# A two-layer hybrid backbone: adaLN pieces in groups run from the last loaded on, and a last projection laid out by tokens

## The chip, the cores and the metric

The kernel runs on one core of a Trainium2 chip. The metric is the time of one execution on the device in microseconds (us); lower is better. PE is the matmul engine (TensorE), DVE is VectorE, ACT is ScalarE, POOL is GpSimd and SP is SyncE; the last two issue nearly all DMAs here.

## The reference

Two layers work on 512 tokens (256 context, 256 latent) of width 2048, all in float32. Per layer, `c @ ada_w` gives a shift, a scale and a gate per feature for latent and context (adaLN); the normed and modulated tokens go through one input projection into three head groups (an S5 state space, attention with 8 heads, an mLSTM), and the joined outputs go through the output projection and are added through the gate. The second layer keeps the latent tokens only, and the result is a final RMSNorm.

```
shift, scale, gate = split(silu(c) @ ada_w[l] + ada_b[l], 3)
xn = rmsnorm(h_lat, norm_w[l]) * (1 + scale) + shift
ya, yb, yc = s5(xn @ w_in), attention(xn @ w_in), mlstm(xn @ w_in)
h_lat = h_lat + gate * (concat([ya, yb, yc]) @ w_out[l])
...
return rmsnorm(h_lat, final_norm_w)
```

## The kernel before

Activations lie with features on the 128 partitions and tokens along the free axis (16 tiles `h` of 128 x 512). Each matmul in the projections is made of three: every weight chunk of 128 x 1024 is loaded by SP (`wchunk`, L178 on, three buffers `raw`), split by ACT into a high part `hi` and by DVE into a rest `lo`, and the activations likewise into `xh` and `xl`; `hi*xh`, `hi*xl` and `lo*xh` are added up in PSUM. A tile scheduler orders the instructions of each engine by priorities; within an engine they run in that order, so one that waits holds up all behind it.

The stages are, in order: the first loads, S5 preparation of layer 0 (`s5_prep`, DVE) and row statistics (`st`, `sp`, `spb` on PE); `inputs` (L1204 on), which makes the modulated tokens two tiles at a time (`make_xn`) and feeds them into the S5 projection (`proj_u`, tiles `pu`), the attention values (`pv`) and the gates (`gps`); `layer`; `out_proj` of layer 0; then the same for layer 1.

The adaLN vectors of layer 0 come from 64 pieces of weights, 512 KB each, in groups of four. POOL loads a piece into one of five buffers `ar` (L287); PE multiplies it by the two-column `cact` into `adps` (`ada_piece`, four matmuls that are eight records in the trace, L159), and after the fourth piece of a group ACT copies the sum out (`aev`) and two small matmuls turn it to columns (`ada_flush`). `ada_step(1)` stands between every three `pu` matmuls, and each call runs one piece. Each piece that is run lets POOL load the next one. The gates of layer 0 are 32 such pieces that run during the attention projections (`ada_open` with `batch=BT0`). The adaLN vectors of layer 1 are made on DVE instead, in the mLSTM stage of layer 0: 64 pieces of 512 KB in two buffers, two multiply-reduces `aj` each (`adv_piece`, L368).

`out_proj` (L1386 on) of layer 1 makes 16 feature tiles of 128 x 256: 48 matmuls of 256 columns each, the weights stationary. Then the gate is applied (`h`), squares are summed over partitions by PE (`st`), and at the end the root of the mean is computed, spread by a matmul (`spb`), and multiplied in before the four output DMAs.

Of the kernel before, what the change touches and what calls it, by code (L numbers as in the profile page):

```python
# [52 lines left out]
BT0 = 1  # L53
# [66 lines left out]
PC = dict(ada_b=(0, 48), nw=(48, 16), cw=(64, 24), cb=(88, 8), mnw=(96, 4), gb=(100, 1), fw=(101, 16), qkw=(117, 2))  # L120
NPC = 119


class Kern:
# [126 lines left out]
    def proj_u(self, l, i, ada):  # L251
# [6 lines left out]
        for kk in range(2):  # L258
            k = 2 * i + kk
            wh, wl = hi[:, kk * 512:kk * 512 + 512], lo[:, kk * 512:kk * 512 + 512]  # L260
            for t in range(4):
# [5 lines left out]
                if ada:  # L267
                    self.ada_step(1)

# [20 lines left out]
    def ada_piece(self, pid):  # L290


        self.ada_flush()
        ps, raw = self.ada_ps, self.ada_raw.pop(pid)
        fine = pid < 64
        pc, last = (pid % 4, 3) if fine else (pid % 16, 15)
        for j in range(4):
            self.mm(ps[32 * j:32 * j + 2, 0:256], self.cact[:, 4 * pc + j if fine else pc],
                    raw[:, j * 256:j * 256 + 256], start=pc == 0, stop=pc == last)
        if pc < last:  # L300
            return
        ev = self.aq["ev"]()
        self.act(ev, ps[:, 0:256], AF.Copy)
        self.apend = (pid, ev)
# [21 lines left out]
    def ada_open(self, pool, bufs, rate, ids, tag="ar", ev=None, batch=1):  # L326
# [3 lines left out]
                       src="ada", run=self.ada_piece)  # L330
        self.ada_fetch()

    def adv_open(self, pool, bufs, rate, ids):
# [3 lines left out]
                       src="adt", run=self.adv_piece)  # L337
# [63 lines left out]
    def ada_next(self):  # L401
        q = self.aq
        q["run"](q["ids"][q["done"]])
# [53 lines left out]
    def make_xn(self, l, pool, hb, rb, ks):  # L457

        xt = []
        for k in ks:  # L460
            t = pool.tile([128, 512], F32, tag="xt", bufs=5, name=self.nm("xt"))
# [33 lines left out]
    def s5_prep(self, l, sp, dp, scratch):  # L495
        V = self.V
        g = self.s5 = {}
        par = sp.tile([128, 112], F32, name=self.nm("spar"))
        self.nc.sync.dma_start(par, self.i["spar"][l])
# [101 lines left out]
        bt = scratch("b", [128, 2, 16, 16])  # L601
        self.nc.sync.dma_start(bt, self.i["sb"][l].rearrange("p (r a q) -> p r a q", r=2, a=16))
# [382 lines left out]
    def ml_gates(self, l):  # L985
# [16 lines left out]
        li = mp.tile([128, 4, 2, 4], F32, tag="ga6", bufs=1, name=self.nm("ga"))  # L1002
# [19 lines left out]
        RQ = mp.tile([128, 128], F32, tag="RQ", bufs=1, name=self.nm("RQ"))  # L1022
        bt = mp.tile([128, 128], F32, tag="bt", bufs=1, name=self.nm("bt"))
# [181 lines left out]
    def inputs(self, l, pool, hb, rb, ada=False):  # L1205
# [3 lines left out]
        xt = []  # L1209
        for i in range(8):  # L1210
            if ada:
                while self.aq["done"] < 8 * i + 8:
                    self.ada_step(1)
                if self.aq["done"] == 8 * i + 8:
                    self.ada_flush()
            ks = (2 * i, 2 * i + 1)
            xt += self.make_xn(l, pool, hb, rb, ks)
            self.proj_u(l, i, ada)
# [17 lines left out]
    def layer(self, l, sp):  # L1236
# [73 lines left out]
        if need:  # L1310
            self.adv_open(mp, 2, ADR, range(0, 64))
# [74 lines left out]
    def out_proj(self, l, hp, beside=lambda: None, side=()):  # L1386

        need = l == 0
        t0 = 0 if need else NCTX
        n = NT - t0  # L1390
        self.pri = 400
        hb, self.hw, sq = [], [], {}

        def group(a):
            for k in range(a, a + 4):
                self.stats_add(k, sq.pop(k), n)

        self.stats_begin()
        for dt in range(KT):
            h = hp.tile([128, 512], F32, tag=f"h{dt}", bufs=1, name=self.nm("h"))  # L1400
            src = self.i["ht"][dt] if need else self.hs[dt]
            self.nc.sync.dma_start(h[:, t0:], src)

            def cb(ps):
                for v, a in ((1, 0), (0, 256)) if need else ((0, 256),):
                    hh = h[:, a:a + 256]
                    self.stt(hh, ps[:, a - t0:a - t0 + 256], self.adG[l][:, dt, v:v + 1], hh, OP.mult, OP.add)
                if need:
                    self.nc.sync.dma_start(self.hs[dt], h[:, 256:512])
                    return  # L1410

            self.pri, self.epri = 400, 400
            self.proj_a((self.i["wo"][l, dt, 0], self.i["wo"][l, dt, 1]), t0, cb)
# [5 lines left out]
            sq[dt] = self.stats_sq(hp, h[:, t0:], n, "xt", 5)  # L1419
            if not need and dt:  # L1420
                self.final_w(hp, hb, dt - 1)
        beside()
        group(12)
        if not need:
            self.final_w(hp, hb, 15)
        return hb

    def final_w(self, hp, hb, dt):
        if dt % 4 == 0:
# [175 lines left out]
```

## Time and profile before

| | |
|---|---|
| median of 3 runs | 1658.59 us (1657.88 to 1662.95) |
| the profiled execution | 1657.79 us |
| its span in the trace | 1656.0 us, so 1.79 us lie around it |
| PE busy | 1588.6 us, 96% of the span |
| DVE, ACT, POOL busy | 73%, 40%, 8% |

The matmuls overlap in the trace (a 512-column one lasts 0.39 us and the next starts 0.23 us later), so a busy PE is not a PE at its peak: the distance between starts tells what a matmul costs. Rows of the timeline give the start and the length in us, the engine, the line, the output and the operands, and how many were merged (`x8`).

### The profile page before, as it was taken

What the parts mean: (1) busy time and instruction counts of PE and PEld (TensorE: products, weight loads), DVE (VectorE), ACT (ScalarE), POOL (GpSimd) and SP (SyncE); (2) the same over time, 40 slices, a digit from 0 to 9 for tenths busy, and PEclk for the clock granted to TensorE, in tenths of its full rate; (3) what the DMA queues carried; (4) which work ended last, traced back from release to release, by engine and by line L of the source; (5) the groups of instructions that cost most, each with busy time, mean ns of one, the idle gap of its engine ahead of it and who ended that gap; (6) DMA issues with size and microseconds to landing.
All of it is one profiled execution on the core that took longest, in us unless ns stands there. A gap on an engine that the chain in (4) does not pass through costs nothing.

```text
span 1656.0 us, 27071 instructions
## 1 busy us (share of the span) xinstructions
PE 1588.6 (96%) x10542; PEld 1346.8 (81%) x10542; DVE 1203.6 (73%) x2545; ACT 669.3 (40%) x1278; POOL 131.2 (8%) x252
## 2 busy tenths in 40 slices
PE   5999999999999899999999999899999999999996
PEld 1567988878768878788887777689989979999996
DVE  5432888777949796999899887556777687557744
ACT  3333344434354344322242323463355453354542
POOL 2221010010000110110000110100000012000000
PEclk9999999999999999999999999899999999999998
DMA  9885244351225665565455555535455458553753
GB/s 378 299 302 175 87 141 168 128 181 52 66 104 165 187 194 179 179 200 183 137 171 168 188 184 171 185 99 165 155 184 172 157 188 279 193 161 118 223 178 112
DMA packets 88033, 288.08 MB, mean 174 GB/s; under 512 B 10208, under 2 KB 18144, under 8 KB 87264
## 3 DMA queue, kind: packets, MB, share of 16 engines
q1 hardware_dynamic: 52704, 158.33, 29.5%
q0 software_dynamic: 35200, 128.01, 23.1%
q8 instruction: 83, 1.36, 0.3%
q14 instruction: 46, 0.38, 0.1%
HBM read 268.44 MB, written 17.86 MB: 173 GB/s over the span
## 4 chain that ended last, share of the span: by engine, by line
PE 61%; DVE 18%; issue 12%; DMA 7%; ACT 2%; POOL 0%; DVEq 0%; POOLq 0%; ACTq 0%
PE pa L159 28%; PE pb L159 9%; PE pu L159 6%; DMA ar<-adt 5%; DVE lo L145 4%; DVE tp L145 3%; PE adps L159 3%; PE psm L159 2%; DMA ar<-ada 2%; DVE aj L368 2%; PE psY L159 2%; PE pv L159 2%; PE psO L159 1%; PE psS L159 1%; DVE S L785 1%
## 5 line engine op out<-in xcount | busy, mean ns | idle before, releaser
L159 PE MATMUL pa<-xh,hi 128*128 128x512 f32 (+1 forms) x1408 | 490.3, 348 | 0.0
L156 ACT ACTIVATE hi<-raw 128x1024 fp32r<-128x1024 f32 x256 | 271.1, 1059 | 539.1 <-PE pa L159 307.4
L159 PE MATMUL pa<-xh,lo 128*128 128x512 f32 (+1 forms) x1408 | 484.6, 344 | 0.0
L159 PE MATMUL pa<-xl,hi 128*128 128x512 f32 (+1 forms) x1408 | 484.4, 344 | 0.0
L145 DVE TENSOR_TENSOR lo<-raw,hi 128x1024 fp32r<-128x1024 f32 x256 | 312.6, 1221 | 143.5 <-ACT hi L156 136.7
L159 PEld LDWEIGHTS pa<-xh,hi 128*128 128x128 f32 x1408 | 266.4, 189 | 34.7 <-issue 5.4
L159 PEld LDWEIGHTS pa<-xh,lo 128*128 128x128 f32 x1408 | 266.7, 189 | 31.1 <-issue 1.9
L159 PEld LDWEIGHTS pa<-xl,hi 128*128 128x128 f32 x1408 | 266.8, 189 | 30.7 <-issue 2.7
L159 PE MATMUL pb<-hi,xh 128*128 128x256 f32 x832 | 241.7, 291 | 0.0
L159 PE MATMUL pb<-lo,xh 128*128 128x256 f32 x832 | 238.3, 286 | 0.0
L159 PE MATMUL pb<-hi,xl 128*128 128x256 f32 x832 | 237.7, 286 | 0.0
L368 DVE CUSTOM_DVE_ANT_0 aj<-ar,cb 128x1024 bf16<-128x1024 f32 x160 | 195.3, 1220 | 33.8 <-DMA ar<-adt 32.5
L159 PEld LDWEIGHTS pb<-hi,xh 128*128 128x128 f32 x832 | 160.1, 193 | 4.4 <-issue 4.1
L159 PEld LDWEIGHTS pb<-lo,xh 128*128 128x128 f32 x832 | 160.3, 193 | 1.9 <-issue 1.0
L159 PEld LDWEIGHTS pb<-hi,xl 128*128 128x128 f32 x832 | 160.1, 192 | 2.0 <-issue 2.0
L287 POOL DMA_DIRECT2D ar<-adt x96 | 50.7, 528 | 545.3 <-DVE adp L368 216.8
L159 PE MATMUL adps<-ar,cact 128*2 128x256 f32 x768 | 67.3, 402 | 18.1 <-DVE cact L145 12.1
L287 POOL DMA_DIRECT2D ar<-ada x96 | 50.7, 529 | 314.7 <-PE adps L159 310.6
L159 PE MATMUL pu<-hi,xh 128*128 128x512 f32 x128 | 56.4, 440 | 4.1 <-ACT xh L156 4.1
L156 ACT ACTIVATE g<-psS,sm 128x512 f32<-128x512 f32 (+1 forms) x48 | 29.3, 611 | 62.9 <-DVE sm L149 62.4
L159 PE MATMUL pu<-lo,xh 128*128 128x512 f32 x128 | 54.5, 426 | 0.0
L159 PE MATMUL pu<-hi,xl 128*128 128x512 f32 x128 | 53.8, 429 | 0.0
(301 smaller groups left out, 2155.9 us busy)
## 6 DMA issues: line engine op xcount, KB each, us to landing
raw<-wa SPq DMA_DIRECT2D x112, 512.0 KB, 3.6
ar<-ada POOLq DMA_DIRECT2D x96, 512.0 KB, 5.1
ar<-adt POOLq DMA_DIRECT2D x96, 512.0 KB, 4.3
raw<-wb SPq DMA_DIRECT2D x64, 512.0 KB, 3.9
raw<-wo SPq DMA_DIRECT2D x64, 512.0 KB, 3.6
raw<-wu SPq DMA_DIRECT2D x16, 512.0 KB, 4.4
h<-ht SPq DMA_DIRECT2D x32, 256.0 KB, 6.0
tb<-E POOLq DMA_DIRECT2D x8, 516.0 KB, 3.2
```

What stands on the lines that cost most here:

```text
L145: return self.V.tensor_tensor(o, a, b, op=op)
L156: return self.S.activation(o, a, f, **kw)
L159: return self.T.matmul(o, w, x, start=start, stop=stop, skip_group_check=True)
L287: self.nc.gpsimd.dma_start(raw, self.i[self.aq["src"]][pid])
L368: self.V.tensor_tensor_reduce(junk, raw, row, 1.0, 0.0, OP.mult, OP.add, self.adp[:, half, kind, dt, v:v + 1])
L785: V.tensor_tensor_scan(f(S[:, ri]), f(dt), f(Z[:, ri]), 0.0, op0=OP.mult, op1=OP.add)
```

## The change

- `ada_open` gets a run order: with `batch=4` each group of four pieces is run back to back, the one loaded last first, and the group's first and last matmul flags follow. Seven buffers take the place of five. The gates of layer 0 run in twos (`BT0 = 2`).
- The first loads are issued in another order (S5 parameters, constants, then the 16 `h`), and they, the opening of the adaLN pieces and `s5_prep` get a higher priority than the statistics.
- `inputs` makes the modulated tokens of step i+1 during step i (`ready`, called from `proj_u`); the buffers of `xt` grow from 5 to 7 (layer 0) and 6 (layer 1).
- The DVE pieces of layer 1's adaLN get a third buffer in layer 0; to make room, three small tiles of the mLSTM gates share others.
- The last output projection is written anew (`out_last`): tokens on partitions, the activations stationary and 512 weight columns moving. The gate row comes from a matmul with ones (`pg`), the residual `hs` is turned by PE (`ph`), squares are summed by ACT along the free axis, and the final weight is a row tile (`fw`).

```diff
-BT0 = 1
+BT0 = 2
+XTB = (7, 6)
@@ proj_u
                 if ada:
                     self.ada_step(1)
+                if kk == 0 and t == 0:
+                    ahead()
@@ ada_piece
-        pc, last = (pid % 4, 3) if fine else (pid % 16, 15)
+        n, b = 4 if fine else 16, self.aq["batch"]
+        pc, first, last = pid % n, b - 1, n - b
...
-                    raw[:, j * 256:j * 256 + 256], start=pc == 0, stop=pc == last)
-        if pc < last:
+                    raw[:, j * 256:j * 256 + 256], start=pc == first, stop=pc == last)
+        if pc != last:
@@ ada_open, ada_next
+        self.aq["order"] = [p for a in range(0, len(ids), batch) for p in reversed(ids[a:a + batch])]
...
-        q["run"](q["ids"][q["done"]])
+        q["run"](q["order"][q["done"]])
@@ inputs
+        def ready(i):
+            if i > 7:
+                return
             if ada:
                 while self.aq["done"] < 8 * i + 8:
                     self.ada_step(1)
...
+            with self.tc.high_priority(60):
+                xn[i] = self.make_xn(l, pool, hb, rb, (2 * i, 2 * i + 1))
+        ready(0)
...
+            self.proj_u(l, i, ada, lambda: ready(i + 1))
@@ layer
-            self.adv_open(mp, 2, ADR, range(0, 64))
+            self.adv_open(mp, 3, ADR, range(0, 64))
@@ out_last (new, in place of out_proj(1), final_w and stats_end)
+        def gate(b):
...
+            self.tt(dg, self.c("I").unsqueeze(1).to_broadcast([128, 4, 128]),
+                    self.adG[1][:, 4 * b:4 * b + 4, 0:1].to_broadcast([128, 4, 128]), OP.mult)
+            pg = self.pS.tile([128, 512], F32, tag="bS", name=self.nm("pg"))
+            self.mm(pg, self.c("ONE"), dg.rearrange("p a c -> p (a c)"))
+            self.act(gr[:, 512 * b:512 * b + 512], pg, AF.Copy)
+        for b in range(4):
...
+            for ch in range(8):
...
+                for t in range(2):
+                    for kk in range(2):
...
+                        self.mm(ps[t], self.xh[k][:, tk], wh, start=k == 0, stop=False)
+                        self.mm(ps[t], self.xh[k][:, tk], wl, start=False, stop=False)
+                        self.mm(ps[t], self.xl[k][:, tk], wh, start=False, stop=k == 15)
...
+                    self.tr(p[:, 128 * q:128 * q + 128], hs[4 * b + q][:, 128 * t:128 * t + 128])
...
+                    self.tt(o, ps[t], gr[:, bs], OP.mult)
+                    self.tt(o, o, pt[t], OP.add)
+                    self.act(sq, o, AF.Square, accum_out=ss[:, t, b:b + 1])
+                    if b < 3:
+                        self.tt(o, o, fw[:, bs], OP.mult)
+        self.V.tensor_reduce(ms, ss, axis=AX.X, op=OP.add)
+        self.ts(ms, ms, 1.0 / D, OP.mult, EPS, OP.add)
+        self.rsqrt(hp, rs, ms, 2)
+        for t in range(2):
+            self.stt(H[t][:, 1536:], H[t][:, 1536:], r, fw[:, 1536:], OP.mult, OP.mult)
+            self.act(H[t][:, :1024], H[t][:, :1024], AF.Copy, scale=r)
+            self.ts(H[t][:, 1024:1536], H[t][:, 1024:1536], r, OP.mult)
...
@@ body
+            with tc.high_priority(1000):
...
+                ids = range(64)
+                self.ada_open(hp, 7, 1.0, ids, batch=4)
+                self.s5_prep(0, s5c, s5c, scratch, loads)
```

The order of PE just ahead of the first `pu` matmul, before (`ar` are adaLN pieces, `st`, `sp` and `spb` the statistics):

```order
L159 MATMUL adps<-ar_410,cact 2x256 x4
L159 MATMUL sp_500<-cst,sev_498 128x2 x4
L159 MATMUL adps<-ar_419,cact 2x256 x4
L159 MATMUL adps<-ar_428,cact 2x256 x4
L159 MATMUL adps<-cst,aev_479 128x2 x2
L159 MATMUL adps<-ar_439,cact 2x256 x4
L159 MATMUL spb_535<-dg_533,cst 128x512
L159 MATMUL adps<-ar_452,cact 2x256 x4
L159 MATMUL adps<-ar_461,cact 2x256 x4
L159 MATMUL adps<-ar_470,cact 2x256 x4
L159 MATMUL pu_574<-hi_580,xh_562 128x512
```

The same place now:

```order
L160 MATMUL st_323<-sq_454,cst 32x512
L160 MATMUL adps<-cst,aev_441 128x2 x2
L160 MATMUL sp_489<-cst,sev_487 128x2 x4
L160 MATMUL adps<-ar_423,cact 2x256 x4
L160 MATMUL adps<-ar_402,cact 2x256 x4
L160 MATMUL adps<-ar_394,cact 2x256 x4
L160 MATMUL adps<-ar_388,cact 2x256 x4
L160 MATMUL spb_539<-dg_537,cst 128x512
L160 MATMUL adps<-cst,aev_483 128x2 x2
L160 MATMUL pu_562<-hi_568,xh_550 128x512
```

Seventeen pieces stood ahead of `spb` and three between it and the first `pu`; now sixteen stand ahead of it, the last four in falling order, and none behind it.

PE during the S5 projection, before:

```order
L159 MATMUL pu_576<-hi_580,xh_562 128x512
L159 MATMUL adps<-ar_481,cact 2x256 x4
L159 MATMUL pu_576<-lo_581,xh_562 128x512
L159 MATMUL pu_576<-hi_580,xl_563 128x512
L159 MATMUL pu_577<-hi_580,xh_562 128x512
L159 MATMUL adps<-ar_490,cact 2x256 x4
L159 MATMUL pu_577<-lo_581,xh_562 128x512
```

And now:

```order
L160 MATMUL pu_563<-hi_673,xh_587 128x512
L160 MATMUL adps<-ar_602,cact 2x256 x4
L160 MATMUL adps<-ar_521,cact 2x256 x4
L160 MATMUL adps<-ar_513,cact 2x256 x4
L160 MATMUL adps<-ar_507,cact 2x256 x4
L160 MATMUL pu_563<-lo_674,xh_587 128x512
```

Behind the first `pu` there were 44 single pieces (29 among `pu`, 13 at `pv`, 2 at `gps`); now there are 12 groups of four (9 among `pu`, 3 among `pv`), the first two 10 `pu` apart, the others some 20 to 30 matmuls of `pu` and `pv`.

PE at the end of the program, before, after the last `pa` of the last feature tile:

```order
L159 MATMUL pa_16152<-xh_15119,lo_16186 128x256
L159 MATMUL st_15129<-sq_16214,cst 32x256
L159 MATMUL sp_16224<-cst,sev_16222 128x2 x2
L159 MATMUL spb_16243<-dg_16241,cst 128x256
L1600 UNCONDITIONAL_BRANCH
```

And now, between the first and the second block of 512 columns (the program ends behind the eight `ph` of the fourth block):

```order
L160 MATMUL po_15168<-hi_15302,xl_15120 128x512
L164 MATMUL ph_15318<-cst,hs_15129 128x128
L164 MATMUL ph_15318<-cst,hs_15131 128x128
L164 MATMUL ph_15318<-cst,hs_15133 128x128
L164 MATMUL ph_15318<-cst,hs_15135 128x128
L164 MATMUL ph_15323<-cst,hs_15129 128x128
L164 MATMUL ph_15323<-cst,hs_15131 128x128
L164 MATMUL ph_15323<-cst,hs_15133 128x128
L164 MATMUL ph_15323<-cst,hs_15135 128x128
L160 MATMUL po_15338<-hi_15342,xh_15059 128x512
```

The statistics left PE, and eight turning matmuls per block came; one `pg` stands in the middle of each block.

## Rows read from the trace of the kernel before

**Rows 1.** Windows by stage: us, busy us of each engine, PE clock, DMA share, GB/s.

```profile
0.00:50.00 50.00, 30.01 (x198) 9.81 (x202) 29.29 (x156) 15.87 (x29) 11.89 (x26) 0.93 0.98 377
50.00:100.00 50.00, 49.47 (x358) 32.15 (x351) 18.98 (x34) 21.64 (x38) 12.91 (x25) 0.97 0.85 287
...
480.00:700.00 220.00, 209.21 (x1170) 177.07 (x1169) 182.56 (x354) 94.24 (x178) 22.70 (x43) 0.98 0.56 176
```

**Rows 2.** Timeline of PE among `pu`, one adaLN piece between.

```profile
61.19 0.40 PE L159 MATMUL pu<-lo,xh 128*128 128x512 f32 x1
...
62.52 0.40 PE L159 MATMUL pu<-hi,xh 128*128 128x512 f32 x1
```

**Rows 3.** Timeline of PE among `pv`, one adaLN piece between.

```profile
76.00 0.28 PE L159 MATMUL pv<-hi,xl 128*128 128x256 f32 x1
...
76.97 0.28 PE L159 MATMUL pv<-lo,xh 128*128 128x256 f32 x1
```

**Rows 4.** Timeline of PE, two adaLN pieces in a row.

```profile
218.22 1.05 PE L159 MATMUL adps<-ar,cact 128*2 128x256 f32 x16
219.20 0.39 PE L159 MATMUL pb<-hi,xh 128*128 128x256 f32 x1
```

**Rows 5.** Timeline of PE, from the spread of the statistics to `pu`.

```profile
47.87 2.08 PE L159 MATMUL spb<-dg,cst 128*128 128x512 f32 x2
...
53.15 0.62 PE L159 MATMUL pu<-hi,xh 128*128 128x512 f32 x1 [0.53 <-ACT xh L156]
```

**Rows 6.** DMAs of `ar`, issue to landing, from 0 to 53 us, then 50 to 150.

```profile
DMA to landing us min/median/max: 4.6/7.3/11.1
...
DMA to landing us min/median/max: 4.0/5.1/8.6
```

**Rows 7.** The chain that ended last, layer 1's `inputs`: start, us, what.

```profile
1058.30 13.91 PE pu L159 x48
1073.20 11.61 PE pu L159 x48
```

**Rows 8.** Waits of DVE and PE from 480 to 870 us: in total, times, longest.

```profile
DVE aj L368 <- DMA ar<-adt: 20.4, 18, 2.7
...
PE psP L163 <- ACT g L156: 8.1, 6, 3.2
```

**Rows 9.** The chain again, runs of `pa`: 512 columns, then twice 256 (layer 1's output).

```profile
837.75 26.58 PE pa L159 x117
...
1540.07 34.64 PE pa L159 x288
1575.28 23.15 PE pa L159 x192
```

**Rows 10.** Timeline of PE, a float32 matmul of 512 columns (two records).

```profile
365.44 1.02 PE L159 MATMUL psS<-kT,qT 128*128 128x512 f32 x2
366.31 0.38 PE L163 MATMUL psT<-cst,g 128*128 128x128 f32 x2
```

**Rows 11.** Timeline of PE, turning matmuls.

```profile
332.78 1.09 PE L163 MATMUL psP<-cst,g 128*128 128x128 f32 x8
333.63 0.36 PE L159 MATMUL pb<-hi,xh 128*128 128x256 f32 x1
```

**Rows 12.** Timeline of the end, from the last `pa`.

```profile
1639.79 0.28 PE L159 MATMUL pa<-xh,lo 128*128 128x256 f32 x1
...
1642.83 0.16 DVE L150 TENSOR_SCALAR ms<-sp 128x2 f32<-128x2 f32 x1 [2.24 <-PE sp L159]
...
1644.99 0.43 DVE L145 TENSOR_TENSOR dg<-cst,rs 128x256 f32<-128x256 f32 x1
...
1648.46 3.79 SPq L1515 DMA_DIRECT2D out<-hw  x4
```

**Rows 13.** Costliest groups by shape: count, busy us and mean ns, idle before.

```profile
L145 DVE TENSOR_TENSOR xt<-h,rb 128x512 f32<-128x512 f32 x32 | 21.0, 686 | 33.8 <-PE gps L159 30.0 <-ACT rb L156 3.7
L156 ACT ACTIVATE sq<-h 128x512 f32<-128x512 f32 x32 | 20.1, 631 | 22.9 <-DMA h<-ht 9.8 <-DVE h L153 9.5 <-PE st L159 3.1
```

More of the change, by code (lines that the diff above doesn't have):

```diff
@@ L249, in drain, with proj_u @@
                     self.streams.remove(st)
-    def proj_u(self, l, i, ada):
+    def proj_u(self, l, i, ada, ahead):
         if i == 0:
@@ L336, in adv_open @@
         self.aq = dict(pool=pool, batch=1, tag="aw", bufs=bufs, rate=rate, ids=list(ids), loaded=0, done=0, credit=0.0,
-                       src="adt", run=self.adv_piece)
+                       src="adt", run=self.adv_piece, order=list(ids))
         self.cb = None
@@ L492, in gate_end, with s5_load, s5_prep @@
         self.V.tensor_copy(self.GS.rearrange("p a b c d -> p (a b c d)"), pt[:, 0:64])
-    def s5_prep(self, l, sp, dp, scratch):
+    def s5_load(self, l, sp, scratch):
+        par = sp.tile([128, 112], F32, name=self.nm("spar"))
+        self.nc.sync.dma_start(par, self.i["spar"][l])
+        bt = scratch("b", [128, 2, 16, 16])
+        self.nc.sync.dma_start(bt, self.i["sb"][l].rearrange("p (r a q) -> p r a q", r=2, a=16))
+        return par, bt
+    def s5_prep(self, l, sp, dp, scratch, loads):
         V = self.V
         g = self.s5 = {}
-        par = sp.tile([128, 112], F32, name=self.nm("spar"))
-        self.nc.sync.dma_start(par, self.i["spar"][l])
+        par, bt = loads
         are, aim, ldt = par[:, 0:32], par[:, 32:64], par[:, 64:96]
@@ L1208, in inputs @@
         self.gate_begin(l, pool)
-        xt = []
-        for i in range(8):
+        xn = {}
+        def ready(i):
+            if i > 7:
+                return
             if ada:
@@ L1213, in inputs @@
                     self.ada_step(1)
-                if self.aq["done"] == 8 * i + 8:
+                if self.apend is not None and self.apend[0] < 8 * i + 8:
                     self.ada_flush()
-            ks = (2 * i, 2 * i + 1)
-            xt += self.make_xn(l, pool, hb, rb, ks)
-            self.proj_u(l, i, ada)
+            with self.tc.high_priority(60):
+                xn[i] = self.make_xn(l, pool, hb, rb, (2 * i, 2 * i + 1))
+        ready(0)
+        xt = []
+        for i in range(8):
+            self.proj_u(l, i, ada, lambda: ready(i + 1))
+            xt += xn.pop(i)
             if ada and i % 2:
@@ L1384, in layer, with out_proj @@
         rag.__exit__(None, None, None)
[L1386 to L1390, printed above, removed]
+    def out_proj(self, hp, beside=lambda: None, side=()):
         self.pri = 400
-        hb, self.hw, sq = [], [], {}
+        hb, sq = [], {}
         def group(a):
             for k in range(a, a + 4):
-                self.stats_add(k, sq.pop(k), n)
+                self.stats_add(k, sq.pop(k), NT)
         self.stats_begin()
@@ L1418, in out_proj @@
                 group(dt - 4)
[L1419 to L1421 removed]
+            sq[dt] = self.stats_sq(hp, h, NT, "xt", XTB[1])
         beside()
         group(12)
[L1424 to L1431 removed]
+        return hb
@@ L1510, in body @@
             gh2, hp = pool("hb1", "right")
-            self.out_proj(1, hp)
-            rb = self.stats_end(hp, NCTX)
-            for k, o in enumerate(self.hw):
-                self.tt(o, o, rb[:, :256].unsqueeze(1).to_broadcast([128, 4, 256]), OP.mult)
-                nc.sync.dma_start(self.o["out"][k], o.rearrange("p k t -> p (k t)"))
+            self.out_last(hp)
             shut(gh2, gx)
@@ L1598 @@
            for n, a in arrays.items()}
-    outs = {"out": nc.dram_tensor("out", (4, 128, 1024), F32, kind="ExternalOutput").ap()}
+    outs = {"out": nc.dram_tensor("out", (2, 128, 2048), F32, kind="ExternalOutput").ap()}
     with tile.TileContext(nc) as tc:
@@ L1603 @@
     o = r.results[0]["out"]
[L1604 removed]
+    return np.ascontiguousarray(o.reshape(256, D))[None]
```

104 lines of the change are left out of this document (68 added, 36 removed).

## The prediction

> **What bounds the kernel now.** I read the windows by stage first, then the timeline of PE inside the stages that the change touches, then the waits and the end of the chain. The windows show three regimes [rows 1]. Up to 50 us DMA is the limit: its share is 0.98 at 377 GB/s while PE works 30 of 50 us. From 50 to 100 us PE is busy 49.47 of 50 us and DMA has slack (287 GB/s). In the mLSTM stage of layer 0, 480 to 700 us, PE idles 220 - 209.21 = 10.8 us. The end is a chain without overlap: behind the last `pa` at 1639.79 us, which lasts 0.28 us, the span goes on for 1656.0 - 1640.1 = 15.9 us [rows 12].
>
> **The groups of four pieces among `pu` and `pv`.** One `pu` matmul costs 11.61/48 = 0.24 us [rows 7], one of 256 columns 23.15/192 = 0.12 us [rows 9]. A single piece between `pu` takes 62.52 - 61.19 = 1.33 us less the two `pu` starts, so 0.85 us [rows 2]; between `pv` 0.97 - 0.24 = 0.73 us [rows 3]. Two pieces in a row take 219.20 - 218.22 = 0.98 us up to the next matmul, and one alone 0.54 us, so each further piece in a row costs about 0.43 us [rows 4]; the rest is the change to other matmuls and back. Before: 29 x 0.85 + 13 x 0.73 + some 1 us for the two at `gps` = 35.1 us. Now 9 groups x (0.85 + 3 x 0.43) + 3 x (0.73 + 3 x 0.43) = 19.3 + 6.1 = 25.4 us, although four more pieces lie here than before. That is -9.7 us on the engine that bounds the stage. The twelve small flushes stay.
>
> **The first `pu`.** Before DMA is full until then, so bytes count. Sixteen pieces instead of seventeen must be there for `spb`: 0.524 MB / 377 GB/s = 1.4 us earlier [rows 1]. But behind the newest of them three more pieces run, 0.43 us each at full clock and twice that at the lower level, at which `spb` ran (2.08 us for two records, against 1.02 us later [rows 5, 10]): 1.3 to 2.6 us. I take +0.5 us, with -1.5 and +2 as ends. The S5 preparation and the 16 `h` ahead gain nothing more here: the last `st` still stands on PE behind the third group, which waits for its twelfth piece. From `spb` to `pu` lie 53.15 - 47.87 = 5.3 us; there PE had three pieces to run and starts `pu` at full pace, now it has one flush. In layer 1, where PE idles ahead of `pu`, the first 48 take 13.91 instead of 11.61 us [rows 7]: +2.3 us taken, between 0 and 2.3.
>
> **Waits for the newest piece.** A group starts with the piece that was loaded last, and the buffer for it came free with the first piece of the group before. Between two group starts lie, for 20 `pu`, 4.7 + 2.15 + one flush of about 0.5 = some 7.2 us; POOL can issue about 0.5 us into it, so a load may take 6.7 us. It took 5.1 us in the median, 8.6 at most, from 50 to 150 us [rows 6]. Behind a waiting piece all of PE is queued, and behind PE the splits of the next chunks. I take +1.5 us for all twelve; 0 is one end, 1.9 us x 12 = 23 us the other. The Trainium skill, "DMA: Bandwidth & Descriptors", section "Anatomy of one DMA — SWDGE (gpsimd) path", fits a DMA issued by GpSimd as 2.0 us plus bytes over 436 GB/s; an estimate from it is 3.2 us for 512 KB, no wait at all, and the sum would be 1.5 us lower. The rows are longer than the page's figure, 4.0 us at least, so they decide.
>
> **The gates of layer 0 in twos.** Of 32 pieces 18 stood in pairs already; seven further merges at 0.54 + 0.2 - 0.43 = 0.31 us [rows 3, 4] give -2.2 us. With two buffers a pair needs its newest load within the distance of two pieces; ends -4 and +2.
>
> **The third buffer of the DVE pieces.** DVE stood 20.4 us in 18 waits for these loads [rows 8], and behind such a wait the softmax sums stand, then `g` on ACT, for which PE waited 8.1 us [rows 8]. A load has one piece more time, so most of the 20.4 us goes; what comes late next is DVE itself, busy 182.56 of 220 us [rows 1]. I take half of PE's 8.1 us: -4.0 us; ends 0 and -10.8. The shared gate tiles and the earlier `make_xn` cost nothing that I can see: PE waited for none of them, and DVE has room from 50 to 100 us.
>
> **The last projection.** 768 matmuls of 256 columns at 0.1206 us are 92.6 us; the gap for `st` between two runs of `pa` is 1575.28 - 1574.71 = 0.57 us [rows 9], three of them 1.7 us: 94.3 us. Now 384 of 512 columns; at 26.58/117 = 0.227 us [rows 9] 87.2 us. Added: four `pg` at 366.31 - 365.44 = 0.87 us [rows 10] plus 0.2 for the change, 4.3 us; three times eight `ph` at 0.85 us [rows 11] plus 0.2, 3.2 us. In all 94.7 us: +0.4 us. The splits on ACT and DVE stay 32 of each and hide as before; the loads of `hs` and `fw` are 3.1 MB in 90 us. The Trainium skill, "TensorE: Matmul & The Clock Gate", section "Back-to-back issue gap", gives N/2.4 + 2.5 ns, so 109 and 216 ns: by it the halved count saves only 1 us, and the sum would be 4.4 us higher. The rows show the larger saving, 5.4 us, and decide, though the operands change sides here.
>
> **The tail.** Behind the last `po`: eight `ph` (0.9 us), beside them the two products with the gate, then two sums of 0.69 us and two squares of 0.63 us [rows 13]; the second sum ends 2.1 us after the last `po`, the second square 2.9. Then the sum over blocks (0.2) and the root, 1644.99 - 1642.83 = 2.2 us [rows 12], give 5.3 us. Four DVE operations of at most 0.69 us give 8.1 us, the last DMA issue follows at 8.8, and from the last issue to the end it was 1656.0 - 1648.46 - 3.79 = 3.75 us [rows 12]. That is 12.5 instead of 15.9 us: -3.4 us.
>
> **Sum.** -9.7 + 0.5 + 2.3 + 1.5 - 2.2 - 4.0 + 0.4 - 3.4 = -14.6 us. The profiled execution of 1657.79 us (1.79 around its span) would become 1643.2 us. It lay 0.8 us below the median of the runs shown, so I forecast 1644.0 us.
>
> **Rivals.**
> - PE's idle time in the mLSTM stage goes whole (10.8 instead of 4.0 us) and no group waits (1.5 us): -14.6 - 6.8 - 1.5 = -22.9, 1635.7 us. For it: the waits of DVE for loads (20.4 us) are larger than all of PE's idle time. Against: DVE is 83% busy there.
> - The third buffer gives PE nothing, because DVE only waits elsewhere: -10.6, 1648.0 us.
> - DMA cannot follow the faster PE. Four pieces and a share of the weight chunks are 2.1 + 0.4 MB per 7.2 us = 346 GB/s; the stage ran at 287. If 300 GB/s is all, a group takes 8.3 us, 1.1 us more, 13.2 instead of 1.5 us over twelve: -2.9 us, 1655.7 us. Against it: 377 GB/s in the first 50 us [rows 1].
> - Slower than before: each of the twelve groups stands 1.9 us for its newest piece (8.6 us to landing, the longest row of [rows 6], which the first 50 us come near with a median of 7.3 us). That is 23 us instead of 1.5: +6.9 us, 1665.5 us. It decides from a landing time of 6.7 us on, and eats the whole gain at 8.0 us.
> - That the change does not do what it says is hardly open for the groups, since PE's order shows them in rows of four.
>
> **How the numbers follow.** About 0.3%, 5 us, is what a measurement of this kernel can tell from no change. Chances: the forecast 0.54, with its own range 1637 to 1652; PE's idle time gone 0.14; no gain from the third buffer 0.15; DMA at 300 GB/s 0.11; the waits for the newest piece 0.06. The first three are faster by over 5 us, the fourth is the same, the last slower. The range from 1632 to 1656 leaves out the slower case and a little below the fastest.
>
> **What would show it.** Right: from the first `pu` to the first `pb` (118 us before) PE's timeline has runs of `adps` of 32 records at 1.7 us and is about 8 us shorter; the waits of DVE for `adt` loads from 480 to 870 us fall below 8 us and PE's idle time there below 9 us; `po` starts lie 0.227 us apart and the span ends 12 to 13 us after the last `po`. Wrong: PE waits for `ar` of over 5 us in the S5 projection, a first `pu` later than 56 us, `po` at 0.24 us or more, or a gap of PE for `hs` or `gr`.

## The result, and the profile after

The changed kernel takes 1638.19 us (median of 4 runs, 1635.15 to 1641.44) against 1658.57 us for the kernel before (4 runs): a ratio of 0.9866, 95% interval 0.9845 to 0.9888. It is 20.4 us faster; 14.6 us were forecast. A second series gave 1639.92 us and 0.9877 [0.9859, 0.9895].

The profiled execution took 1638.10 us with a span of 1636.0 us (before: 1656.0 us). The windows by stage of the changed kernel, which answer to [rows 1] (us, then busy us of PE, PEld, DVE, ACT and POOL, granted clock, DMA share, GB/s):

```profile
0.00:50.00 50.00, 28.61 (x181) 9.14 (x182) 30.28 (x156) 15.69 (x28) 12.28 (x27) 0.87 0.95 363
...
480.00:700.00 220.00, 213.05 (x1208) 181.85 (x1207) 192.44 (x352) 90.18 (x168) 23.85 (x45) 0.98 0.57 184
```

These windows cut at fixed times, so they mix stages that have moved against each other. To see where the time went, I read the same six points out of PE's timeline in both profiles and took differences:

| stretch | before, us | after, us | difference | forecast |
|---|---|---|---|---|
| start to first `pu` | 53.15 | 54.34 | +1.2 | +0.5 |
| first `pu` to first `pb` | 118.23 | 108.29 | -9.9 | -5.9 (groups -9.7, cold start +2.3, waits +1.5) |
| first `pb` to first `psG` | 294.95 | 291.05 | -3.9 | -2.2 |
| first `psG` to `spb` of layer 1 | 586.37 | 579.62 | -6.8 | -4.0 |
| `spb` of layer 1 to its last `pb` | 379.67 | 381.92 | +2.3 | 0 |
| last `pb` to the end | 223.63 | 220.78 | -2.9 | -3.0 |
| sum | 1656.00 | 1636.00 | -20.0 | -14.6 |

The groups in the timeline of PE (start, us, instruction; compare [rows 2, 4]): four pieces now run as one block of 32 records and take 61.75 - 59.91 = 1.84 us up to the next matmul. The forecast's own figures, 0.54 for the first and 0.43 us for each further piece, give 1.83.

```profile
59.91 1.91 PE L160 MATMUL adps<-ar,cact 128*2 128x256 f32 x32
61.75 0.63 PE L160 MATMUL pu<-hi,xl 128*128 128x512 f32 x1
```

The end of the start in PE's timeline, answering to [rows 5]. PE waits 4.43 us for the last squares, runs the fourth group at the lower clock, and between `spb` and `pu` has one flush to run and idles for 2.86 us. The first eight `pu` then start 0.43 us apart (the first two 0.61) instead of 0.23:

```profile
35.85 1.06 PE L160 MATMUL st<-sq,cst 128*32 128x512 f32 x1 [4.43 <-ACT sq L157]
...
45.72 3.59 PE L160 MATMUL adps<-ar,cact 128*2 128x256 f32 x32 [2.61 <-DVE Ec L146]
49.24 1.90 PE L160 MATMUL spb<-dg,cst 128*128 128x512 f32 x2
50.98 0.50 PE L160 MATMUL adps<-cst,aev 128*128 128x2 f32 x4
54.34 0.81 PE L160 MATMUL pu<-hi,xh 128*128 128x512 f32 x1 [2.86 <-ACT xh L157]
54.95 0.63 PE L160 MATMUL pu<-lo,xh 128*128 128x512 f32 x1
55.38 0.63 PE L160 MATMUL pu<-hi,xh 128*128 128x512 f32 x1
```

DMAs of `ar`, from 0 to 53 us and from 50 to 150, answering to [rows 6]; the median is above that of before in both stretches, and still no `adps` waits for one between 54 and 170 us:

```profile
DMA to landing us min/median/max: 4.4/7.5/14.6
...
DMA to landing us min/median/max: 3.8/6.3/8.6
```

POOL issues these loads in fours, one behind the other, and the first of four lands soonest. Of the four issued from 60.9 to 62.4 us the first took 3.9 and the last 6.8 us:

```profile
DMA to landing us min/median/max: 3.9/5.1/6.8
```

Waits of DVE and PE from 480 to 870 us (in total, times, longest), answering to [rows 8]. DVE's 20.4 us fall to 0.8, PE's 8.1 us at `psP` to 0.2, and a single wait of PE of 6.6 us is new:

```profile
DVE aj L375 <- DMA ar<-adt: 0.8, 1, 0.8
...
PE pa L160 <- DVE mt L154: 6.6, 1, 6.6
PE psP L164 <- ACT g L157: 0.2, 1, 0.2
```

Two shorter waits of PE in the kernel before, from 460 to 860 us, are gone as well:

```profile
PE psm L159 <- DVE mt L153: 2.7, 1, 2.7
...
PE psh L163 <- DVE mt L145: 1.7, 2, 1.5
```

The last stage in the chain that ended last, answering to [rows 9] (start, us, what), and the end of the timeline, answering to [rows 12]:

```profile
1528.88 10.92 PE po L160 x48
1539.80 0.86 PE pg L160 x2
1540.66 10.90 PE po L160 x48
1551.55 0.87 PE ph L164 x8
```

```profile
1621.86 0.39 PE L160 MATMUL po<-hi,xl 128*128 128x512 f32 x1
...
1630.21 1.19 SPq L1504 DMA_DIRECT2D out<-H  x1
```

A `po` is 10.92/48 = 0.2275 us. From the last `po`, which another matmul follows at 1622.09, to the end are 13.9 us.

### The profile page after: what moved, and what is told of

Read it like the earlier page. It is cut to its first block, busy times and chain, and to the rows that moved or that the text cites. A ratio compares the mean times of both kernels' runs of the same rounds, so it can differ in the third digit from the quotient of the medians.

```text
span 1636.0 us, 26259 instructions
## 1 busy us (share of the span) xinstructions
PE 1567.7 (96%) x10160; PEld 1330.1 (81%) x10160; DVE 1208.3 (74%) x2555; ACT 665.5 (41%) x1266; POOL 131.4 (8%) x252
## 4 chain that ended last, share of the span: by engine, by line
PE 53%; issue 13%; DVE 11%; DMA 7%; ACT 1%; POOL 1%; POOLq 0%; DVEq 0%; ACTq 0%
PE pa L160 28%; PE po L160 5%; DMA ar<-ada 4%; PE pb L160 4%; PE pu L160 3%; DVE lo L146 3%; DMA ar<-adt 2%; PE psm L160 2%; PE psO L160 1%; PE psS L160 1%; PE psG L160 1%; PE psY L160 1%; PE psP L164 1%; DVE aj L375 1%; POOL ar L291 1%
## 5 line engine op out<-in xcount | busy, mean ns | idle before, releaser
L160 PE MATMUL pa<-xh,hi 128*128 128x512 f32 (+1 forms) x1152 | 419.4, 364 | 6.6 <-DVE mt L154 6.6
L160 PE MATMUL pa<-xh,lo 128*128 128x512 f32 (+1 forms) x1152 | 413.5, 359 | 0.0
L160 PE MATMUL pa<-xl,hi 128*128 128x512 f32 (+1 forms) x1152 | 412.5, 358 | 0.0
L160 PEld LDWEIGHTS pa<-xh,hi 128*128 128x128 f32 x1152 | 218.4, 190 | 41.2 <-issue 11.9
L160 PEld LDWEIGHTS pa<-xl,hi 128*128 128x128 f32 x1152 | 218.7, 190 | 30.6 <-issue 2.7
L160 PEld LDWEIGHTS pa<-xh,lo 128*128 128x128 f32 x1152 | 218.4, 190 | 30.4 <-issue 1.3
L160 PE MATMUL adps<-ar,cact 128*2 128x256 f32 x768 | 54.7, 400 | 4.4 <-DVE Ec L146 2.6
L160 PEld LDWEIGHTS pu<-hi,xh 128*128 128x128 f32 x128 | 39.9, 312 | 15.0 <-ACT xh L157 8.1
```

The source lines that it names most:

```text
L160: return self.T.matmul(o, w, x, start=start, stop=stop, skip_group_check=True)
```

## The experiments

Each kernel below was timed together with the kernel before, so the ratio to before is the measure; the changed kernel's own are 0.9866 and 0.9877. An interval is about 3 us to either side. The stretches of one profile can be sharper, because what happens elsewhere in the execution does not enter; all are in this table (starts in PE's timeline, us):

| kernel | ratio to before, interval | first `pu` | first `pb` | first `psG` | `spb` L1 | last `pb` | span |
|---|---|---|---|---|---|---|---|
| changed, again | 0.9877 [0.9859, 0.9895] | 54.48 | 163.01 | 453.62 | 1033.67 | 1415.53 | 1636.4 |
| 1 singles | 0.9904 [0.9885, 0.9922] | 53.08 | 170.54 | 460.92 | 1039.57 | 1424.03 | 1644.9 |
| 2 loading order | 0.9912 [0.9893, 0.993] | 52.63 | 168.49 | 461.78 | 1039.84 | 1420.82 | 1641.6 |
| 3 two `aw` buffers | 0.9953 [0.9935, 0.9972] | 53.42 | 164.53 | 455.64 | 1054.39 | 1435.17 | 1656.0 |
| 4 `az` singles | 0.9892 [0.9873, 0.9911] | 54.32 | 163.95 | 458.66 | 1037.08 | 1419.07 | 1639.9 |
| 5 before + third `aw` | 0.997 [0.9959, 0.9982] | 54.83 | 173.12 | 468.13 | 1046.14 | 1428.07 | 1651.6 |
| 6 old last stage | 0.9886 [0.9869, 0.9903] | 53.18 | 163.51 | 454.16 | 1034.16 | 1415.63 | 1639.3 |
| 7 new start | 0.9853 [0.9835, 0.9871] | 49.94 | 156.89 | 448.17 | 1028.02 | 1409.98 | 1630.8 |
| 8 no step ahead | 0.9878 [0.9861, 0.9896] | 55.16 | 163.46 | 454.12 | 1033.46 | 1416.29 | 1637.1 |
| 9 four `ar` buffers | 1.0072 [1.0055, 1.0088] | 52.99 | 193.26 | 483.89 | 1063.20 | 1449.79 | 1670.6 |
| 10 new start, pieces later | 0.984 [0.982, 0.986] | 50.49 | 157.10 | 448.53 | 1028.18 | 1413.87 | 1634.7 |

The changed kernel again:

> The changed kernel itself once more, beside the others of this call: 1637 to 1641 us, a ratio near 0.987. It is the mark that the others of this call are compared with; where the same stretches differ between its two profiles, that is the spread of one profile.

Up to the last `pb` its profile differs from the first one by at most 0.4 us at any point. How much a stretch tells differs from stretch to stretch. Over the kernels that share its code, the new last stage, from the last `pb` to the end, lies within 0.1 us, first `pb` to first `psG` within 1.1 (290.38 to 291.43), the mLSTM stage with three buffers within 2.1 (578.01 to 580.05), and first `pu` to first `pb` with the groups and the changed start within 2.8 (108.29 to 111.11). The first `pu` itself comes at 53.15 and 54.83 us in the two kernels with the old start (before and kernel 5), and at 52.63 to 55.16 us in those with the changed one.

The stretch from `spb` of layer 1 to the last `pb`, in which these kernels do nearly the same work, runs from 379.67 us (before) to 386.59 us (kernel 9) over the profiles. Kernel 5, which differs there from the kernel before by the shared tiles alone, takes 381.93 us. So the +2.3 us of the first table need not come from the change; as the kernel before has the lowest of all thirteen, whether some of it does stays open. The profiles of kernels 1, 3 and 10 are of their slowest execution, 3.3, 5.4 and 4.1 us above the median, so their spans lie above what the ratios tell.

**1. The groups undone.**

```diff
-                self.ada_open(hp, 7, 1.0, ids, batch=4)
+                self.ada_open(hp, 7, 1.0, ids)
```

> The changed kernel with layer 0's 64 pieces run one at a time again; everything else stays. Theory A (a piece alone among `pu` or `pv` costs some 0.15 us of interruption, which groups of four save): the stretch from the first `pu` to the first `pb` goes from 108.3 us back to some 118, and the time from 1638.2 to about 1648. Rival B (the stretch is shorter because the inputs are made a step ahead, the groups matter little): the stretch stays at 108 to 110 us and the time at 1638 to 1640.

Theory A for the stretch: 117.46 us instead of 108.29. The windows of the `adps` instructions alone, from first `pu` to first `pb`, before, then after, then in this kernel (columns as above without POOL's; the first count is PE's records):

```profile
53.15:171.38 118.23, 34.49 (x400) 11.84 (x400) 1.93 (x12) 4.58 (x12) 1.00 0.72 244
```

```profile
54.34:162.63 108.29, 29.11 (x432) 15.86 (x432) 2.10 (x13) 4.62 (x12) 0.98 0.73 263
```

```profile
53.08:170.54 117.46, 34.88 (x408) 12.39 (x408) 1.94 (x12) 4.62 (x12) 0.98 0.71 242
```

More records in fewer microseconds of PE: that is the saved change of matmuls, and the `pu` or `pv` that starts behind each block saves the rest. In the whole time less arrives: 5.1 us slower than the changed kernel by the median (1643.29 against 1638.19), 0.0027 to 0.0038 by the ratios, 4.5 to 6.3 us. The first `pu` comes 1.3 us earlier without groups, which gives part of it back, and the first `pb` 7.9 us later. Against the other profiles with the same groups (kernels 3, 4 and 6, 109.63 to 111.11 us in the stretch) the difference is 6.4 to 7.8 us. So the groups are worth 6 to 9 us here; the 9.2 of one pair of profiles is the upper end.

**2. The groups kept, each in the order of loading.**

```diff
-        self.aq["order"] = [p for a in range(0, len(ids), batch) for p in reversed(ids[a:a + batch])]
+        self.aq["order"] = list(ids)
-        pc, first, last = pid % n, b - 1, n - b
+        pc, first, last = pid % n, 0, n - 1
```

> The changed kernel with each group run in the order of loading, first piece first; the groups stay. Theory A (seven buffers run ahead of the pieces, no `adps` waits for `ar` in the changed kernel, so it does not matter which piece of a group comes first): 1638.2 within 1.5 us, the same 108.3 us from the first `pu` to the first `pb`. Rival B (newest first keeps a group together, in loading order a late piece splits it): up to 12 groups x 0.3 us, so 1640 to 1642, and matmuls of `adps` that wait for `ar`.

I expected no difference, and was wrong: 115.86 us in the stretch and a ratio like that of singles. (The edit reaches the gates' twos too: behind the first `pa` three pairs fall apart, and first `pb` to first `psG` is 293.30 instead of 291.05 us.) Rival B is right that newest first keeps a group together, but not in its mechanism, since no piece waits. PE's timeline of this kernel shows what happens:

```profile
58.05 0.61 PE L160 MATMUL adps<-ar,cact 128*2 128x256 f32 x8
58.60 0.63 PE L160 MATMUL pu<-hi,xh 128*128 128x512 f32 x1
...
59.86 0.61 PE L160 MATMUL adps<-ar,cact 128*2 128x256 f32 x8
60.40 0.63 PE L160 MATMUL pu<-lo,xh 128*128 128x512 f32 x1
```

The four pieces are issued together in the code, but stand one by one with up to five `pu` between them in PE's order. My reading, which the order bears out but no run took apart, is that the scheduler puts an instruction where it reckons its inputs to be there: in loading order the pieces become ready one after the other; newest first, the first piece is ready last, and the other three are ready with it, so they fall into one block. What is shown is that the reversal is not a detail of the groups: without it there are none.

**3. Two `aw` buffers in the changed kernel**, and **5. the third one alone in the kernel before** (with the three small scratch tiles shared, for which there would be no room otherwise).

```diff
-            self.adv_open(mp, 3, ADR, range(0, 64))
+            self.adv_open(mp, 2, ADR, range(0, 64))
```

> The changed kernel with two `aw` buffers in layer 0's mLSTM stage instead of three. Theory A (the third buffer takes away DVE's waits for `adt` pieces, and PE waited for DVE behind them): DVE's `aj` waits for DMA come back at 10 us or more, PE idle time there goes up by 4 to 6 us, 1642 to 1645. Rival B (the buffer gives nothing, the stage is set by DVE's work in any case): the `aj` waits come back and the time stays at 1638 to 1639.5.

> The kernel before with the third `aw` buffer of layer 0's mLSTM stage alone (and the three small scratch tiles shared that make room for it); pieces one at a time, old last stage. Theory A (taking the buffer out of the changed kernel cost 14 us, so it is worth about as much by itself): DVE's `aj` waits fall from 20.4 us to under 2, the stretch from the first `psG` to the first `spb` of layer 1 falls from 586.4 us to some 575, and the time to 0.992 to 0.994 of the kernel before. Rival B (the forecast's -4.0 holds in the kernel before, and the 14 us come from how the rest of the change and two buffers go together): the stretch falls by 3 to 5 us and the time is 0.997 to 0.998 of before.

The kernel before gains 5.4 us by the median (1654.15 against 1659.52, a ratio of 0.997 as in rival B of the second expectation); its stage falls by 8.4 us to 578.01, between rival B's 3 to 5 and theory A's 11. The changed kernel loses far more: 12.5 to 14 us, and its stage rises by 19.1 us to 598.75 in a profile that is 5.4 us above this kernel's median. Kernel 3 against [rows 8], waits from 460 to 860 us:

```profile
DVE aj L375 <- DMA ar<-adt: 17.1, 18, 3.2
...
PE pa L160 <- DVE mt L154: 6.6, 1, 6.6
PE psP L164 <- ACT g L157: 5.7, 2, 5.0
PE psm L160 <- DVE mt L154: 3.5, 1, 3.5
PE psh L164 <- DVE mt L146: 2.7, 2, 2.5
```

The windows of the whole stage, in the kernel before, in the changed kernel and in kernel 3:

```profile
466.33:1052.70 586.37, 567.56 (x2959) 462.62 (x2958) 499.97 (x1066) 210.14 (x363) 49.77 (x95) 0.99 0.54 173
```

```profile
453.68:1033.30 579.62, 565.02 (x2960) 460.07 (x2958) 499.69 (x1066) 209.49 (x363) 49.41 (x93) 0.99 0.54 175
```

```profile
455.64:1054.39 598.75, 572.42 (x2959) 465.23 (x2958) 501.73 (x1066) 209.50 (x363) 49.34 (x93) 0.98 0.52 170
```

Against the changed kernel PE idles 26.3 instead of 14.6 us, 11.7 more, and the same matmuls take 7.4 us longer at a granted clock of 0.98 instead of 0.99. PE works 19.3 instead of 4.9 us of this stage at the lower level (0.50); half of the difference, an estimate of 7.2 us, is what that costs. Two things make it worse than the kernel before was, where PE idled 18.8 us: the 6.6 us wait of the new order is there and the old waits come on top, and with them more time at the lower clock. Kernels 3 and 5 both have the 6.6 us wait and the kernel before has not, so it does not hang on the number of buffers; that it comes from the shared scratch tiles, which 3 and 5 have in common, was not tried by itself. DVE's order shows what it is: four `aj` stand ahead of the first product with `pa`, which starts 37.3 us behind the first `psG`; in the kernel before none does, and it starts at 29.8. Kernel 10 takes the wait away and leaves the tiles shared.

**4. The gates one by one.**

```diff
-BT0 = 2
+BT0 = 1
```

> The changed kernel with the 32 `az` pieces of layer 0's attention stage run one at a time instead of in twos. Theory A (16 interruptions of some 0.14 us come back): +2.2 us, 1640.4. Rival B (with two buffers a pair waits for its second piece, so the pairs save nothing or cost): 1637 to 1638.5.

First `pb` to first `psG` is 294.71 instead of 291.05 us, 3.7 more, and the time 3.5 us above the changed kernel's median. Theory A with a larger number than the 2.2 us. Up to the first `pa` it is 181.37 instead of 179.21 us, and from there to the first `psG` 1.5 us more. Both are the forecast's term: in PE's order eight single pieces stand ahead of the first `pa` where the changed kernel has four more pairs, and six behind it where it has three. That makes seven merges, as forecast, at 0.52 us each instead of 0.31.

**6. The old last stage in the changed kernel**: layer 1's `out_proj`, `final_w` and the last statistics as in the kernel before.

```diff
-            self.out_last(hp)
+            self.out_old(1, hp)
+            rb = self.stats_end(hp, NCTX)
...
```

> The changed kernel with layer 1's output projection, final norm and output as in the kernel before (token columns, 16 projections of N = 256, rows of statistics). Theory A (the forecast's sum: +0.4 of PE against a tail 3.4 us shorter): 3.0 us slower than the changed kernel, a ratio to before near 0.9885. Rival B (the new stage is all PE time: 384 matmuls of 512 columns at 0.2275 us against 768 of 256 at 0.1206, gates and transposes on top, and the tail of 13.7 us is no shorter in effect): within 1 us of the changed kernel, 0.986 to 0.987.

From the last `pb` to the end 223.67 instead of 220.78 us: 2.9 us, theory A. The median says 2.0 us, which agrees within its interval.

**8. The inputs made in the step that uses them.**

```diff
-            self.proj_u(l, i, ada, lambda: ready(i + 1))
-            xt += xn.pop(i)
+            xt += self.make_xn(l, pool, hb, rb, ks)
+            self.proj_u(l, i, ada)
```

> The changed kernel with the inputs made in the step that uses them, as before, instead of one step ahead. Theory A (PE was busy 99.6 per cent of that stage already in the kernel before, so the step ahead buys little): within 1.5 us of the changed kernel, ratio 0.986 to 0.9875, first `pu` to first `pb` 108 to 110 us. Rival B (groups of four put the last piece that an input needs right ahead of it, and without the step ahead each of the 8 steps waits for VectorE and ScalarE): PE idle of 1 to 2 us at most steps between 55 and 165 us, 6 to 10 us slower, ratio 0.990 to 0.9925.

108.30 us in the stretch, 1638.84 us: the step ahead is worth nothing that can be measured.

**9. Four `ar` buffers instead of seven.**

```diff
-                self.ada_open(hp, 7, 1.0, ids, batch=4)
+                self.ada_open(hp, 4, 1.0, ids, batch=4)
```

> The changed kernel with four `ar` buffers in layer 0 instead of seven, so that a group's loads can only start when the group before it has run. It puts the forecast's slower rival (each of the groups among `pu` and `pv` waits 1.9 us for its newest piece, +23 us) on trial. Theory A (seven buffers are what keeps that wait at nothing: with four, a group runs each 9 to 10 us, its four loads are issued in 2 us, move 2 MB in 5 to 6 us at some 400 GB/s and land 3 to 4 us after, so the newest piece is late by 0 to 3 us): `adps` waits for `ar` at most groups, 10 to 25 us from first `pu` to first `pb` on top of 108, 1650 to 1663 us. Rival B (the loads are quick enough even so, and the wait was never near): within 3 us of the changed kernel.

Slower than before, as in the forecast's slower rival, and beyond theory A's range: 1671.28 us, 33 us over the changed kernel. The windows from first `pu` to first `pb`, and the issue of two groups' loads on POOL:

```profile
52.99:193.26 140.27, 126.20 (x885) 90.19 (x885) 35.68 (x60) 42.19 (x71) 26.19 (x50) 0.93 0.62 226
```

```profile
96.84 2.09 POOL L291 DMA_DIRECT2D ar<-ada  x4 [7.94 <-PE adps L160]
106.86 2.09 POOL L291 DMA_DIRECT2D ar<-ada  x4 [7.93 <-PE adps L160]
```

A group comes every 10.0 us: its four loads are issued in 2.1 us behind the group before and land 5.5 us later in the median. Each of the twelve later groups starts 0.1 to 2.7 us after its fourth load has landed, so the loads set the pace. Of PE's 14.1 us of idle time, though, only 1.2 are put down to `ar`. The others are waits for the inputs and weights that stand behind the late pieces, as `gps`:

```profile
100.36 1.04 PE L160 MATMUL gps<-xt,wg 128*32 128x512 f32 x2 [0.99 <-ACT xt L157]
...
119.27 1.44 PE L160 MATMUL gps<-xt,wg 128*32 128x512 f32 x2 [1.45 <-ACT xt L157]
```

Busy time is 126.20 against 108.29 us for one group more (1.84 us), so about 16 us are longer work, and they have two causes. The clock explains some 8 of them, by an estimate: PE works 19.0 instead of 3.3 us at the lower level (the clock falls there again at 119.8, 140.3, 160.8 and 181.2 us, each time behind a wait of 1.45 us for `xt`), and half of the difference is lost. The rest is mostly `gps`. In the changed kernel its matmuls stand in rows of up to eight, here mostly in twos, and two take as long as eight; this is the whole of `gps` in both stretches, then a row of eight in the changed kernel:

```profile
54.34:162.63 108.29, 5.23 (x32) 0.76 (x32) 0.00 (x0) 0.98 0.73 263
```

```profile
52.99:193.26 140.27, 14.72 (x32) 1.68 (x32) 0.00 (x0) 0.93 0.62 226
```

```profile
114.18 1.07 PE L160 MATMUL gps<-xt,wg 128*32 128x512 f32 x8
```

The waits on `ar`, which the forecast named as the sign, would not have shown any of this.

**7. A new start.** In the changed kernel's ACT timeline the split of the first `wu` chunk stands ahead of the last two squares and waits for its DMA:

```profile
29.70 0.63 ACT L157 ACTIVATE sq<-h 128x512 f32<-128x512 f32 x1 [0.61 <-PE st L160]
34.22 1.06 ACT L157 ACTIVATE hi<-raw 128x1024 fp32r<-128x1024 f32 x1 [3.90 <-DMA raw<-wu]
35.18 1.13 ACT L157 ACTIVATE sq<-h 128x512 f32<-128x512 f32 x2
```

As I read it, the squares stand so late because their two buffers come free with PE's `st` (the wait in the first line). So:

```diff
-XTB = (7, 6)
+XTB = (6, 6)
-                self.stats_add(k, self.stats_sq(hp, hb[k], NT, "sq", 2), NT)
+                self.stats_add(k, self.stats_sq(hp, hb[k], NT, "sq", 3), NT)
-            rb = self.stats_end(hp, NT, lambda: self.ada_step(2))
+            with tc.high_priority(3000):
+                rb = self.stats_end(hp, NT, lambda: self.ada_step(2))
```

> The changed kernel with another start: a third buffer for the squares of layer 0's statistics (taken from `xt`, 6 instead of 7), so that no `hi` of `wu` stands ahead of the last two squares on ScalarE, and the end of the statistics scheduled ahead of S5 preparation and of the fourth group of pieces. Theory A (PE loses 4.4 us at the last squares, 1.6 us in the interleaved rsqrt and 1.5 us by a group ahead of `spb`, and DMA has room after 55 us): first `pu` at 47 to 50 us instead of 54.3, first `pb` earlier by as much, 4 to 6 us faster than the changed kernel, a ratio near 0.9835. Rival B (DMA feeds the first 160 us at its limit, and PE meets the wait again at the pieces): first `pu` earlier but first `pb` within 1.5 us of 162.6, with matmuls of `adps` waiting for `ar`; ratio 0.986 to 0.987.

1633.69 us, 0.9853. First `pu` 4.4 us earlier, first `pb` 5.7, the span 5.2 us shorter: theory A, at its slow end for `pu`, though the ratio lies between the two theories. The start in PE's timeline:

```profile
37.81 3.59 PE L160 MATMUL adps<-ar,cact 128*2 128x256 f32 x32 [3.81 <-DMA ar<-ada]
...
44.34 2.05 PE L160 MATMUL spb<-dg,cst 128*128 128x512 f32 x2 [1.42 <-DVE dg L146]
46.32 3.23 PE L160 MATMUL adps<-ar,cact 128*2 128x256 f32 x32
49.94 0.62 PE L160 MATMUL pu<-hi,xh 128*128 128x512 f32 x1 [0.39 <-ACT xh L157]
50.40 0.40 PE L160 MATMUL pu<-lo,xh 128*128 128x512 f32 x1
50.63 0.40 PE L160 MATMUL pu<-hi,xh 128*128 128x512 f32 x1
```

The fourth group now lies behind `spb`, in the time that PE idled, and behind the first one the `pu` start 0.23 us apart at once. The third group now waits 3.8 us for its load, up to 37.8 us, and the end of the statistics comes behind it; rival B's limit is there, ahead of the first `pu` and not behind it.

**10. The same, with the first `adt` pieces held back** by a credit of -3 in `adv_open`.

> The start of the run before last (a third buffer for the squares, the end of the statistics first) and the first `adt` pieces of layer 0's mLSTM stage held back by three pieces of credit. In the changed kernel PE waits 6.6 us for VectorE at the start of that stage, where four `aj` of 1.2 us, the conversion of `cb` and the scans of the gates stand ahead of the first convolution, which frees the `pa` accumulators. Theory A (that wait comes from the first pieces being run ahead of the convolution): PE's 6.6 us wait goes, the stretch from first `psG` to the first `spb` of layer 1 falls by 5 to 7 us to 573 to 575, 4 to 6 us faster than the run with the new start alone, 1628 to 1630 us. Rival B (VectorE is 85 per cent busy there and the pieces only move: the wait comes back at the next product, or the pieces crowd the end): the stretch stays at 578 to 581 and the time at 1633 to 1636.

The 6.6 us wait goes, as A says, but the stage keeps 579.65 us (579.85 in kernel 7): rival B. PE's waits from 460 to 860 us:

```profile
PE pa L160 <- ACT xh L157: 3.6, 1, 3.6
PE psh L164 <- DVE mt L146: 1.6, 2, 1.4
PE psg L164 <- ACT g L157: 1.2, 1, 1.2
```

The three add up to 6.4 us, and PE idles 14.2 us in the stage against 14.7 in kernel 7: the same time under other names. 1632.38 us is no better than kernel 7 within the intervals. Kernels 7 and 10 beat both kernels given; against the changed one kernel 7 gains 2 to 4 us by the ratios, 4.5 to 6 by the medians and 5.2 to 5.6 by the profiles, kernel 10 4 to 6, 6 to 7.5 and, with 385.69 us in layer 1 and the slowest of its five executions profiled, 1.3 to 1.7.

## Why the prediction was right, and where its sizes were off

The change acts where the forecast put it, and each term has the sign that it was given, but for the start and layer 1, whose differences lie within the spread. The 5.4 us by which the table's -20.0 exceeds the -14.6 come from three stretches that gained more than forecast, first `pu` to first `pb` (4.0 us), the gates (1.7) and the mLSTM stage (2.8); layer 1 and the start took 3.0 back.

- **Groups: right in kind, at most a little too large.** Forecast were -9.7 us for the groups and -5.9 for the stretch; measured are -9.9 in the stretch, of which kernel 1 gives 6 to 9 us to the groups. The price of a block came out as forecast (1.84 against 1.83 us). What I did not see: that the reversal makes the blocks (kernel 2). I had read it off PE's order without asking why.
- **Cold start of `pu`: right, a little smaller.** The first eight `pu` start 0.43 us apart instead of 0.23, 1.6 us against the forecast's 2.3, at a granted clock of 0.50. Kernel 7 removes it.
- **First `pu`: +1.2 us, inside -1.5 to +2, but no proof of the +0.5.** The point moves by as much between kernels with the same start, and the new order of the first loads was not tried by itself. The reason given holds in part: the group in front of `spb` runs 3.6 us at the lower clock. But the largest loss, 4.4 us at the last squares, I called a wait for the third group's pieces. It is an ACT instruction in the wrong place; only with that out of the way (kernel 7) does the third group wait for its load, 3.8 us.
- **Waits for the newest piece: 0, forecast +1.5.** The loads came later than I took them, 6.3 us in the median. My 6.7 us between issue and need were about right (some 6.2 us in the trace; the 12 groups start over 79 us). But with seven buffers the load that counts is the first of the four that POOL issues in a row, and the median that I set against it is over all four. By the trace the first landed after 3.8 to 5.7 us and 0.2 to 2.5 us ahead of its group, the fourth after 6.8 to 8.6 us. So the term is 0 for a reason that I did not give, and the margin is small. In kernel 9 the fourth load counts, and the groups wait for it. The estimate of 3.2 us that I made from the Trainium skill, "DMA: Bandwidth & Descriptors", section "Anatomy of one DMA — SWDGE (gpsimd) path", is also off here: the shortest load took 3.8 us.
- **Gates in twos: -3.9, forecast -2.2**, inside its ends; kernel 4 gives 3.7. The seven merges were counted rightly and priced too low, 0.31 instead of 0.52 us.
- **Third buffer: the mis-sized term.** -6.8 us in the stage, forecast -4.0; undoing it costs 12.5 to 14 us in the time. I priced PE's waits at `psP` alone by half. They went almost whole, with those at `psm` and `psh`, some 12 us in all, but the new wait of 6.6 us took the place of half of that: PE's idle time in the stage fell from 18.8 to 14.6 us. That these 4.2 us are the forecast's 4.0 is luck. The other 2.5 us, which the sum had no term for, are the same matmuls in less time; PE works 4.9 instead of 8.7 us at the lower clock, which explains some 1.9 of them. I also put the shared tiles at nothing; kernels 3 and 5 share them and have the new wait, but whether the tiles bring it stays open.
- **Last projection and tail: -2.9, forecast -3.0**, by luck: two errors cancel. The projection is 0.8 us shorter instead of 0.4 longer, since the change from `po` to `ph` and `pg` does not cost the 0.2 us that I took for it; the tail is 13.9 instead of 12.5 us: the last issue comes 8.1 us behind the last `po` and takes 1.2, and from there to the end it is 4.6 us instead of 3.75.
- **Rivals.** PE's idle time gone whole (1635.7 us) came nearest in the number but not in kind: PE still idles 7 us of its window (480 to 700 us). DMA at 300 GB/s did not bind: the stage ran at 366 GB/s between 90 and 108 us.

## What to carry to other kernels

When small side jobs are strung between the matmuls that bound a stage, bundle them, and look in the engine's own order whether they stay together: with the scheduler used here, the item that becomes ready last had to be the first of the bundle. Buy the buffers that let the bundle's loads run ahead before bundling; four instead of seven turned a gain of 20 us into a loss of 11. And price a wait by all that stands behind it in its queue and by the clock after it, not by its own length; then ask which wait will come last once it is gone.

## What the runs showed of the hardware

- Gaps cost twice. With two `aw` buffers 11.7 us of idle time came with 7.4 us of longer matmuls, about what PE's work at the lower clock explains; with four `ar` buffers 14.1 us came with some 8 us of this kind. The granted clock of the start shows both levels: 0.50 from 45 to 50 us, 1.2 of 2.4 GHz, where four pieces take 3.59 us instead of 1.91.
- Eight `gps` matmuls in a row, of 32 output rows each, take 1.07 us, and two take 1.04: in the trace four of them start within 0.03 us, then the other four. Pulled apart into twos, the same 32 matmuls take 14.72 us instead of 5.23, some of that at the lower clock.
- Of four 512 KB loads that GpSimd issues in a row, 0.53 us apart, the first landed after 3.8 to 5.7 us and the fourth after 6.8 to 8.6 us.
- Nearly the same work of layer 1 took between 379.67 and 386.59 us over thirteen profiles, a spread of 7 us, while the end of the program repeated to 0.1 us. A gain of 3 us can be seen in a stretch of a profile before the total shows it, but only in a stretch whose own spread is known to be smaller.
- A change of matmuls does not cost the same everywhere: a lone piece among `pu` costs some 0.3 us besides its own time, `pg` and `ph` among `po` none that can be seen.
